# Weight chunks split by two DMA transfers instead of by GpSimd

## The chip, the cores and the metric

The kernel runs on one core of a Trainium2 chip. The metric is device microseconds of one execution, the median over runs; lower is better. The engines are TensorE (PE; its weight loads are listed as PEld), VectorE (DVE), ScalarE (ACT), GpSimd (POOL) and SyncE (SP), each with its own instruction queue. Before the change only SP issues DMA transfers.

## The reference

512 tokens of width 1024 go through three blocks in float32. The first is a gMLP layer with a SwiGLU FFN (hidden width 2816). The second is a FoX attention layer (16 heads of 64, causal softmax with forget gates) with another such FFN. The third is a block of a chunkwise mLSTM beside attention over the 128 best keys of an indexer, then a per-layer-embedding gate and a last norm. Each layer's modulation vectors come from products of `silu(c)` with wide `ada` matrices. Cut to one FFN, which stands for all the large products:

```python
def swiglu(h, w_gu, w_down):
    gu = h @ w_gu
    g, u = jnp.split(gu, 2, axis=-1)
    return (jax.nn.silu(g) * u) @ w_down
```

## The kernel before, in words

**Products in three passes.** A float32 operand f is split exactly into hi, which is f rounded to float32r, and lo = f - hi. A product is then hi*hi + hi*lo + lo*hi, three TensorE instructions (`mm3`, L416 to L418). Activations are split once, when they are transposed to feature-major tiles (`to_T`: ACT at L407, DVE at L408 and L409). Weights are split as they come.

**Weight chunks.** All weight matrices are laid out on the host in chunks of 128 partitions by 1024 columns, 512 KB each. `wsplit` (L273) brings one chunk: `load_w` issues a transfer from SP into a tile `raw` (L271; four buffers), ACT copies it into `whi` with rounding (L279), and a subtraction gives `wlo` (L282). There are four buffers of `whi` and four of `wlo`. A chunk is used in 24 products of 512 columns, and then its `whi` and `wlo` buffers come free. With `share=n` every n-th chunk, by a running count over the whole kernel, has its subtraction on GpSimd and not on DVE; `share=0` means never. 293 chunks go through `wsplit`, 124 of them with the subtraction on GpSimd.

**Where the shares are.** `gemm_a` keeps weights stationary, `gemm_b` keeps activations stationary. In `gemm_a` with `group=4`, the first four chunks go by halves of the tokens (products of 256 columns), since the second half of the tokens is ready later; `gshare=1` puts all four on GpSimd. This is so at the start of both FFNs (gate and up weights `w_gu`, 44 chunks each; afterwards every second chunk in the first FFN, every third in the second) and of the indexer projection `w_ix`. In `gemm_b` with `tail`, the last chunks of a product are held together and used token tile by token tile, so that the first token tiles are finished early; with `head` the whole first group goes so (the last projection, `w_pg`, with `hshare=1`). Values and queries of the FoX layer (`w_vv`, `w_q`) have `share=1`, as have all chunks that `between` places among the attention's steps, and `w_az` and `w_mo`.

**What else uses raw and GpSimd.** Columns of the modulation vectors (`ada`) are loaded into `raw` as well, and DVE multiplies them by `silu(c)` and sums (L302). `fill` places these loads between the chunks; in the first FFN it is two for each chunk from the eleventh on. In the start of the kernel the `ada` columns have tiles of their own (`d`), and DVE, ACT, PE and SP follow an order written out by hand (`manual_schedule`); some chunks are loaded ahead there and given to `wsplit` as `raw=`. Of the chunks with GpSimd's share, four have such a `raw`. GpSimd also adds relative biases and masks to the attention's score tiles (L1132, L1336, L1408), two heads ahead of their use.

**What sets the order.** Outside the part ordered by hand a planner orders the instructions of each queue by its own estimate of when each is ready, in program order among those that are ready. A buffer is taken when the instruction that writes it first is placed. Each queue then runs strictly in that order, and semaphores hold an instruction until its inputs are there.

Of the kernel before, what the change touches and what calls it, by code (L numbers as in the profile page):

```python
"""One-core Trainium2 kernel: a gMLP layer, a FoX attention layer (each with a SwiGLU FFN), then an
mLSTM + indexer-sparse-attention block with a per-layer-embedding gate, for 512 tokens of width 1024.

Large products run as three float32r passes over exactly split operands (hi*hi + hi*lo + lo*hi).
"""
# [55 lines left out]
# ------------------------------------------------------------------ host layout  # L61
def _wa(w):
    """[K, N] -> [N/128, 128 (k in tile), K/128 * 128]: stationary chunks of 128 outputs."""
    k, n = w.shape
    return np.ascontiguousarray(
        w.reshape(k // P, P, n // P, P).transpose(2, 1, 0, 3).reshape(n // P, P, (k // P) * P))


def _wb(w):
    """[K, N] -> [N/512, K/256, 128, 2 * 512]: moving chunks of two k tiles by 512 outputs."""  # L70
# [29 lines left out]
def layout(i):  # L100
# [33 lines left out]
    # gMLP  # L134
# [14 lines left out]
    # FoX  # L149
# [8 lines left out]
    # second block  # L158
# [3 lines left out]
    # rows of the last tile: keys 0-63, input gates 64-67, forget gates 96-99, indexer weights 100-107  # L162
# [28 lines left out]
# ------------------------------------------------------------------ kernel body  # L191
def body(tc, nc, a):
    V, S_, G, PE = nc.vector, nc.scalar, nc.gpsimd, nc.tensor

    with ExitStack() as es:
# [55 lines left out]
        # ---------------- constants  # L251
# [14 lines left out]
        # ---------------- weights: load, split  # L266
# [7 lines left out]
        def wsplit(src, n=1024, share=0, alloc=None, raw=None):  # L274
            """share: every share-th low part on GpSimd"""
            if raw is None:
                raw = load_w(src, n)
            hi, lo = [alloc(F32R) if alloc else tile_of(pw, q, F32R, 1024) for q in ("whi", "wlo")]
            S_.activation(hi[:, 0:n], raw[:, 0:n], AF.Copy)  # L279
            lo_n[0] += 1  # L280
            e = G if share and lo_n[0] % share == 0 else V
            e.tensor_sub(lo[:, 0:n], raw[:, 0:n], hi[:, 0:n].bitcast(F32))  # L282
            return hi, lo

        # ---------------- modulation vectors, worked off between weight chunks
# [21 lines left out]
        def fill(n=1):  # L307
            """one column's load, and the product for the one loaded before"""
# [25 lines left out]
        def gain(csc, gname):  # L334
            """gain * (1 + scale), a column per feature tile"""
# [5 lines left out]
        def gb_row(cg, gname):  # L341
            """gate * gain, on every partition"""
# [13 lines left out]
        # ---------------- norms, transposes  # L356
        def rsq(out, ss, scale):
            """out = 1 / sqrt(ss * scale + eps)"""
            S_.activation(out, ss, AF.Sqrt, bias=epsc[0:out.partition_size(), :], scale=scale)
            V.reciprocal(out, out)  # L360

        def norm_rows(xr, out):
            """out = xr / rms(xr), a token tile in two halves"""
# [8 lines left out]
        def to_T(ts, xn, g, sh, hi, lo, js=range(KD), spill=None):  # L372
            """token-major halves of the tiles ts -> feature-major hi, lo; what is transposed goes
            to spill as well"""
# [39 lines left out]
        # ---------------- products  # L414
# [5 lines left out]
        def gemm_a(h, w, n, evac, m=P, group=0, nfill=0, share=0, gshare=1):  # L420
            """out^T tile i (m outputs by 512 tokens), weights stationary. The first group goes by
            halves of the tokens, since the second half of h comes later."""
# [20 lines left out]
        def gemm_b(h, w, groups, kt, evac, head=False, tail=0, nfill=0, share=0, raws=(), hshare=1):  # L443
            """out tile (g, t): 128 tokens by 512 outputs, activations stationary. The last chunks
            of a group (all of them in the first with head) go token tile by token tile."""
# [25 lines left out]
        def chunks_a(h, w, n, evac):  # L471
            """gemm_a's weight chunks for between(): source, number of steps, step"""
# [15 lines left out]
        def chunks_b(h, w, g, kt, evac):  # L488
            """gemm_b's weight chunks of a group for between()"""
# [17 lines left out]
        def between(chunks, share=1):  # L507
            """products to be placed between the steps of something else: a function that emits the
            next n steps (all that are left without n)"""
# [1107 lines left out]
```

## Time and profile before

| what | value |
|---|---|
| median of 2 runs | 1943.34 us (1941.35 to 1945.34) |
| profiled execution: span, first to last instruction | 1936.7 us (no other time is given for it) |
| mean granted TensorE clock | 0.982 of full speed |
| PE / PEld busy | 1880.1 us (97%) / 1523.1 us (79%) |
| DVE / ACT / POOL busy | 1123.1 us (58%) / 794.6 us (41%) / 375.8 us (19%) |
| DMA | 299.46 MB, mean 155 GB/s, 45.3% of 16 engines' span |

Busy times are sums over one profiled execution; matmuls are pipelined, so PE counts as busy as long as one is under way. The granted clock is the share of 2.4 GHz that the chip gave TensorE in a stretch; its lower level is 1.2 GHz, 0.50. The DMA share is the mean busy share of the core's 16 DMA engines. "Landing" is the time from a transfer's issue to its completion.

### The profile page before, as it was taken

The numbers are of one execution on the slowest core, as the hardware profiler recorded it, in microseconds if no ns is written. First come the engines' busy times: TensorE is split into PE (matmuls) and PEld (weight loads), VectorE is DVE, ScalarE is ACT, GpSimd is POOL, SyncE is SP. The second block draws the span as 40 slices with busy tenths as digits, with TensorE's granted clock in tenths as the row PEclk, the third lists the DMA queues.
The fourth block names the chain that finished last, engine by engine and source line by source line (L and its number), as shares of the span: only waits on it lengthen the run. The fifth ranks groups of instructions, "written<-read, shape, count | busy, mean of one in ns | idle before, by whom it ended". The sixth has DMA issues, their size and how long they took to land.

```text
span 1936.7 us, 23791 instructions
## 1 busy us (share of the span) xinstructions
PE 1880.1 (97%) x8688; PEld 1523.1 (79%) x8688; DVE 1123.1 (58%) x2132; ACT 794.6 (41%) x1395; POOL 375.8 (19%) x216
## 2 busy tenths in 40 slices
PE   7999998999999999999998999999989999999998
PEld 5788877888878877877777888888876877888887
DVE  7879735677762275367757333322365967856534
ACT  5334324422231255477655222222344246455334
POOL 2100123222220013433322111100020353022011
PEclk9999999999999999999998999999987999999999
DMA  8674753477763446733512322233243633322522
GB/s 330 235 274 137 251 194 109 147 265 260 260 219 109 141 138 205 247 120 126 172 67 97 112 94 96 98 109 126 103 136 98 187 129 111 115 93 88 191 96 100
DMA packets 106191, 299.46 MB, mean 155 GB/s; under 512 B 11893, under 2 KB 14749, under 8 KB 106074
## 3 DMA queue, kind: packets, MB, share of 16 engines
q1 hardware_dynamic: 106074, 297.94, 45.3%
q8 instruction: 69, 1.13, 0.2%
q14 instruction: 48, 0.39, 0.1%
HBM read 266.35 MB, written 34.16 MB: 155 GB/s over the span
## 4 chain that ended last, share of the span: by engine, by line
PE 78%; DVE 11%; DMA 7%; issue 2%; ACT 2%; POOL 0%; SPq 0%; DVEq 0%; ACTq 0%
PE acc L416 22%; PE acc L418 22%; PE acc L417 22%; DMA raw<-in_ada 6%; DVE raw L302 3%; PE tp L975 2%; PE tp L1016 2%; DVE d L302 1%; PE tp L1001 1%; PE tp L974 1%; DVE h L408 1%; PE tp L384 1%; DVE wlo L282 1%; DVE h L409 1%; PE tp L815 1%
## 5 line engine op out<-in xcount | busy, mean ns | idle before, releaser
L279 ACT ACTIVATE whi<-raw 128x1024 fp32r<-128x1024 f32 x293 | 309.9, 1059 | 679.4 <-PE acc L418 305.5
L282 POOL TENSOR_TENSOR wlo<-raw,whi 128x1024 fp32r<-128x1024 f32 x124 | 305.1, 2464 | 1368.3 <-ACT whi L279 1189.1
L417 PE MATMUL acc<-h,whi 128*128 128x512 f32 (+1 forms) x1112 | 418.2, 376 | 10.5 <-DVE h L409 10.4
L416 PE MATMUL acc<-h,whi 128*128 128x512 f32 (+1 forms) x1112 | 418.6, 376 | 5.5 <-DVE h L408 5.2
L418 PE MATMUL acc<-h,wlo 128*128 128x512 f32 (+1 forms) x1112 | 417.5, 375 | 3.3 <-DVE wlo L282 2.7
L282 DVE TENSOR_TENSOR wlo<-raw,whi 128x1024 fp32r<-128x1024 f32 x169 | 212.4, 1259 | 312.6 <-ACT whi L279 312.2
L417 PEld LDWEIGHTS acc<-h,whi 128*128 128x128 f32 x1112 | 212.5, 191 | 48.6 <-DVE h L409 12.7
L416 PE MATMUL acc<-whi,h 128*128 128x512 f32 x608 | 242.5, 399 | 7.9 <-DVE h L408 6.5
L416 PEld LDWEIGHTS acc<-h,whi 128*128 128x128 f32 x1112 | 212.8, 191 | 43.2 <-DVE h L408 6.0
L418 PEld LDWEIGHTS acc<-h,wlo 128*128 128x128 f32 x1112 | 212.7, 191 | 41.9 <-DVE wlo L282 4.5
L417 PE MATMUL acc<-wlo,h 128*128 128x512 f32 x608 | 240.0, 395 | 3.2 <-DVE wlo L282 3.2
L418 PE MATMUL acc<-whi,h 128*128 128x512 f32 x608 | 240.8, 397 | 0.0
L302 DVE SCALAR_TENSOR_TENSOR raw<-raw,cact 128x1024 f32<-128x1024 f32 x96 | 148.9, 1562 | 75.4 <-DMA raw<-in_ada 69.8
L416 PE MATMUL acc<-whi,s 128*128 128x512 f32 (+1 forms) x488 | 190.4, 390 | 0.7 <-DVE t L1308 0.7
L417 PE MATMUL acc<-wlo,s 128*128 128x512 f32 (+1 forms) x488 | 190.7, 391 | 0.0
L418 PE MATMUL acc<-whi,s 128*128 128x512 f32 (+1 forms) x488 | 190.2, 390 | 0.0
L416 PEld LDWEIGHTS acc<-whi,h 128*128 128x128 f32 x608 | 115.5, 190 | 34.2 <-DVE h L408 7.6
L417 PEld LDWEIGHTS acc<-wlo,h 128*128 128x128 f32 x608 | 115.2, 189 | 27.0 <-DVE wlo L282 4.1
L418 PEld LDWEIGHTS acc<-whi,h 128*128 128x128 f32 x608 | 115.2, 189 | 26.5 <-DVE h L409 2.4
L416 PEld LDWEIGHTS acc<-whi,s 128*128 128x128 f32 x488 | 91.7, 188 | 20.1 <-DVE t L1308 1.1
L417 PEld LDWEIGHTS acc<-wlo,s 128*128 128x128 f32 x488 | 91.7, 188 | 18.8
L418 PEld LDWEIGHTS acc<-whi,s 128*128 128x128 f32 x488 | 91.7, 188 | 18.6
(349 smaller groups left out, 2416.4 us busy)
## 6 DMA issues: line engine op xcount, KB each, us to landing
raw<-in_ada SPq DMA_DIRECT2D x96, 512.0 KB, 4.3
raw<-in_w_gu SPq DMA_DIRECT2D x88, 512.0 KB, 3.5
raw<-in_w_dn SPq DMA_DIRECT2D x44, 512.0 KB, 3.2
scr<-t SPq DMA_DIRECT2D x60, 256.0 KB, 4.1
raw<-in_w_o SPq DMA_DIRECT2D x20, 512.0 KB, 3.4
row<-scr SPq DMA_DIRECT2D x36, 256.0 KB, 3.4
d<-in_ada SPq DMA_DIRECT2D x16, 512.0 KB, 6.9
raw<-in_w_v SPq DMA_DIRECT2D x16, 512.0 KB, 5.2
```

The costliest lines, as they stand in the source:

```text
L279: S_.activation(hi[:, 0:n], raw[:, 0:n], AF.Copy)
L282: e.tensor_sub(lo[:, 0:n], raw[:, 0:n], hi[:, 0:n].bitcast(F32))
L302: V.scalar_tensor_tensor(raw, raw, 1.0, cact[0], ALU.mult, ALU.mult, accum_out=modc[:, col:col + 1])
L384: PE.transpose(src[:, i * P:(i + 1) * P], xn[t][j // 4][:, (j % 4) * P:(j % 4 + 1) * P], ident[:])
L408: V.tensor_copy(hi[j][:, c], fj)
L409: V.tensor_sub(lo[j][:, c], fj, hi[j][:, c].bitcast(F32))
L416: PE.matmul(out, lh, rh, start=start, stop=False)
L417: PE.matmul(out, lh, rl, start=False, stop=False)
L418: PE.matmul(out, ll, rh, start=False, stop=stop)
L815: PE.matmul(sp[:, n * P:(n + 1) * P], vt[n, i // 4][:, o], rows[i // 4][:, o], start=True, stop=True)
L975: PE.matmul(sp[:, o:o + w], qs_[me, qs], kl[me, 0:w], start=False, stop=True)
L1016: PE.matmul(po[:, s * P:512], vd[s, hd // 4][:, hq * P:(hq + 1) * P], pt[:, PTO[s]:PTO[s] + n], start=(q == 0 and s == 0), stop=(q == 1 an ...
```

## The change

In `wsplit`, a chunk of GpSimd's share that has no `raw` given is no longer loaded by SP. GpSimd issues a transfer from DRAM straight into `whi`, from float32 to float32r. ACT then writes -hi into `wlo`. GpSimd issues a second transfer of the same chunk that adds it onto `wlo`, which leaves f - hi. No `raw` tile is taken for such a chunk. A chunk with `raw` given has its subtraction on DVE whatever its share, and so has every chunk outside the share. All other lines of the diff drop comments.

```diff
         def wsplit(src, n=1024, share=0, alloc=None, raw=None):
-            """share: every share-th low part on GpSimd"""
+            hi, lo = [alloc(F32R) if alloc else tile_of(pw, q, F32R, 1024) for q in ("whi", "wlo")]
+            lo_n[0] += 1
+            if share and lo_n[0] % share == 0 and raw is None:
+                G.dma_start(hi[:, 0:n], src)
+                S_.activation(lo[:, 0:n], hi[:, 0:n].bitcast(F32), AF.Copy, scale=-1.0)
+                G.dma_start(lo[:, 0:n], src, accum_op=ALU.add)
+                return hi, lo
             if raw is None:
                 raw = load_w(src, n)
-            hi, lo = [alloc(F32R) if alloc else tile_of(pw, q, F32R, 1024) for q in ("whi", "wlo")]
             S_.activation(hi[:, 0:n], raw[:, 0:n], AF.Copy)
-            lo_n[0] += 1
-            e = G if share and lo_n[0] % share == 0 else V
-            e.tensor_sub(lo[:, 0:n], raw[:, 0:n], hi[:, 0:n].bitcast(F32))
+            V.tensor_sub(lo[:, 0:n], raw[:, 0:n], hi[:, 0:n].bitcast(F32))
             return hi, lo
```

## Rows read from the trace of the kernel before

**Rows 1.** The page, busy times and shares of the span.
```profile
PE 1880.1 (97%) x8688; PEld 1523.1 (79%) x8688; DVE 1123.1 (58%) x2132; ACT 794.6 (41%) x1395; POOL 375.8 (19%) x216
```

**Rows 2.** The page, the chain of waits by line.
```profile
PE acc L416 22%; PE acc L418 22%; PE acc L417 22%; DMA raw<-in_ada 6%; DVE raw L302 3%; PE tp L975 2%; PE tp L1016 2%; DVE d L302 1%; PE tp L1001 1%; PE tp L974 1%; DVE h L408 1%; PE tp L384 1%; DVE wlo L282 1%; DVE h L409 1%; PE tp L815 1%
```

**Rows 3.** Groups by line: busy us, mean ns, idle before and its releasers.
```profile
L282 POOL TENSOR_TENSOR wlo<-raw,whi 128x1024 fp32r<-128x1024 f32 x124 | 305.1, 2464 | 1368.3 <-ACT whi L279 1189.1 <-DVE t L394 134.5 <-issue 18.0
```

**Rows 4.** Timeline of ACT, second FFN (start us, duration us).
```profile
1082.02 1.06 ACT L279 ACTIVATE whi<-raw 128x1024 fp32r<-128x1024 f32 x1 [3.84 <-PE acc L417]
...
1087.46 1.06 ACT L279 ACTIVATE whi<-raw 128x1024 fp32r<-128x1024 f32 x1 [3.89 <-issue]
```

**Rows 5.** The tile raw, 375 to 565 us: its transfers' landing.
```profile
DMA to landing us min/median/max: 3.2/4.4/6.1
```

**Rows 6.** The page, DMA issues: KB each, median us to landing.
```profile
d<-in_ada SPq DMA_DIRECT2D x16, 512.0 KB, 6.9
```

**Rows 7.** Stages, POOL at L282: start:end, length, busy, count; clock, DMA share, GB/s.
```profile
75.00:320.00 245.00, 27.93 (x11) 0.99 0.59 203
345.00:565.00 220.00, 50.29 (x20) 1.00 0.70 240
742.00:800.00 58.00, 21.55 (x9) 1.00 0.77 247
1045.00:1270.00 225.00, 31.12 (x13) 1.00 0.28 96
```

**Rows 8.** Timeline of DVE, first 75 us.
```profile
22.32 2.23 DVE L708 TENSOR_TENSOR modc<-modc,vecs 128x1 f32<-128x1 f32 x1
...
26.79 1.22 DVE L302 SCALAR_TENSOR_TENSOR d<-d,cact 128x1024 f32<-128x1024 f32 x1
...
29.54 1.23 DVE L282 TENSOR_TENSOR d<-raw,d 128x1024 fp32r<-128x1024 f32 x1
...
62.90 3.40 DVE L302 SCALAR_TENSOR_TENSOR d<-d,cact 128x1024 f32<-128x1024 f32 x1
```

**Rows 9.** Timeline of ACT, group starts and ends, and the last projection.
```profile
321.56 1.09 ACT L279 ACTIVATE whi<-raw 128x1024 fp32r<-128x1024 f32 x1
...
357.74 1.06 ACT L279 ACTIVATE whi<-raw 128x1024 fp32r<-128x1024 f32 x1 [1.34 <-issue]
...
1027.47 1.09 ACT L279 ACTIVATE whi<-raw 128x1024 fp32r<-128x1024 f32 x1
...
1065.78 1.06 ACT L279 ACTIVATE whi<-raw 128x1024 fp32r<-128x1024 f32 x1 [1.34 <-issue]
...
1401.90 1.06 ACT L279 ACTIVATE whi<-raw 128x1024 fp32r<-128x1024 f32 x1
...
1441.08 1.06 ACT L279 ACTIVATE whi<-raw 128x1024 fp32r<-128x1024 f32 x1 [0.58 <-issue]
...
1879.87 1.06 ACT L279 ACTIVATE whi<-raw 128x1024 fp32r<-128x1024 f32 x1 [0.59 <-PE acc L418]
```

**Rows 10.** Timeline of PE, first products of a group and of the last projection.
```profile
1030.47 0.28 PE L416 MATMUL acc<-h,whi 128*128 128x256 f32 x1
...
1882.95 0.48 PE L416 MATMUL acc<-whi,s 128*128 128x512 f32 x1
```

**Rows 11.** Stretches: length, busy of PE, PEld, DVE, ACT, POOL; clock, DMA share, GB/s.
```profile
1036.00:1042.00 6.00, 2.54 (x10) 1.93 (x10) 5.50 (x6) 2.11 (x6) 4.82 (x2) 0.50 0.80 300
425.00:521.00 96.00, 96.00 (x425) 79.51 (x424) 74.75 (x95) 24.51 (x32) 19.29 (x8) 1.00 0.76 261
```

**Rows 12.** Timeline of POOL, first FFN; nine more such rows lie between.
```profile
424.58 2.39 POOL L282 TENSOR_TENSOR wlo<-raw,whi 128x1024 fp32r<-128x1024 f32 x1 [8.88 <-ACT whi L279]
...
546.22 2.40 POOL L282 TENSOR_TENSOR wlo<-raw,whi 128x1024 fp32r<-128x1024 f32 x1 [9.97 <-ACT whi L279]
```

**Rows 13.** Timeline of SP, before the second FFN.
```profile
1004.45 6.35 SPq L271 DMA_DIRECT2D raw<-in_w_gu  x2
1015.33 19.00 SPq L553 DMA_DIRECT2D scr<-hm  x5
```

## The prediction, made before the result was known

> **What bounds the kernel now.** I read the busy times first, then the chain of waits, the groups by line, and the stages one by one. TensorE (PE) is busy 1880.1 of 1936.7 us [rows 1], and the chain is mostly its three passes L416 to L418 [rows 2]: 57 us of idle time, plus what a lowered clock costs, is all that any change could give back. GpSimd's 124 subtractions of L282 take 2464 ns each, 305.1 us, yet GpSimd spends 1189.1 us waiting for ScalarE (ACT) [rows 3]; its speed is not the bound. What the reader is to see is where weights are needed soon after a buffer comes free. In steady stages ACT refills a whi buffer every 1087.46 - 1082.02 = 5.44 us [rows 4]: that is TensorE's time for one chunk (24 products). With four whi buffers, a chunk whose buffer has just come free is needed three chunks later, 3 x 5.44 = 16.3 us. Today 1.06 us of ACT [rows 4] and 2.46 us of GpSimd (3.5 us) follow the release, because the load went ahead into raw. After the change both transfers come after the release. So the prediction compares one chain with 16.3 us, and looks at four places that have no such lead.
>
> **The change, part by part.** The sum is made against the profiled execution (span 1936.7 us). The page gives no other time for it; the median of the two timed runs is 6.6 us above the span, and I add the sum to the median. All of the 124 low parts leave GpSimd: 120 become two transfers, and the four with a raw tile given go to VectorE (DVE).
>
> *The chain.* Neither a rounding transfer nor an accumulating one, nor any transfer issued by GpSimd, is in the trace. The nearest rows are 512 KB loads: landing 3.2 / 4.4 / 6.1 us (least, median, most) in the first FFN [rows 5], 6.9 us for the median of the crowded start [rows 6]. For the first transfer I take 4.4, since it moves what a load moves (bounds 3.2 and 6.9). The second reads the chunk from DRAM and the tile from SBUF, so I take two loads, 8.8 (bounds: one fast load, 3.2; two of the slowest, 13.8). ACT's copy stays at 1.06 us. Chain: 4.4 + 1.06 + 8.8 = 14.3 us, bounds 7.5 and 21.8. At 14.3 it fits into 16.3: **nothing** is lost in the steady stages, and this cover is 2 us thin. Where it fails, each us over the lead costs 53 us, since 11 + 20 + 9 + 13 = 53 such chunks run at full pace [rows 7].
>
> By the fit in the Trainium skill (DMA: Bandwidth & Descriptors, Anatomy of one DMA), 2.0 us plus bytes at 436 GB/s, a 512 KB transfer would take 3.2 us, an estimate, and the chain would be the 7.5 of my lower bound. This trace shows 3.2 us only as the least landing, and for SyncE's queue, so I do not take it.
>
> *Start of the kernel: gain.* DVE orders the first 70 us (four products L302 per feature tile). A product that meets a GpSimd subtraction takes 3.40 us, otherwise 1.22; a one-column add took 2.23 [rows 8]. There are five such meetings, the add being the first and the product of 3.40 the last: 4 x 2.18 + some 2.1 = 10.8 us. Three subtractions of 1.23 us come to DVE there (chunks with raw given; a fourth falls where DVE waits for PE). Net **-7.1 us** (bounds -10.8 and 0: the two chunks that become transfers may be late).
>
> *Three group starts (both FFNs and the indexer projection).* Four chunks, all GpSimd's, follow a tail that holds all four whi buffers to its end. In the second FFN the first buffer is refilled at 1027.47 [rows 9], TensorE wants it at 1030.47 [rows 10], and the group ends at 1065.78 [rows 9]. Today four subtractions stretch DVE's work there, TensorE is busy 2.54 of 6 us in one stretch and is granted a clock of 0.50 in it, 1.2 instead of 2.4 GHz [rows 11]. After: the first low part at 1027.47 + 14.3 = 1041.8, eight half chunks of 2.72 us = 21.8, and 3 us for another such stretch of 6 us at half the clock: 1066.6, so +0.8. In the first FFN 321.56 + 39.1 = 360.7 against 357.74: +3.0; in the indexer 1401.90 + 39.1 = 1441.0 against 1441.08: -0.1 [rows 9]. Together **+3.7 us** (bounds -17 and +26: three times the chain's bounds). The DVE stretching that goes is inside this sum: what is late next is the low part.
>
> *The last projection's head.* TensorE starts it at 1882.95 [rows 10] and reaches the second chunk six products of 0.23 us later; that chunk's buffer is refilled at 1879.87 [rows 9]. Low part at 1894.2, stall 9.9 us plus 3 us of clock: **+12.9 us** (bounds +3 and +20). Here I count no stretched DVE work that would pay it back.
>
> *DMA time.* At a share of 0.76 and 261 GB/s [rows 11] 96 us move 47.8 loads, so one load costs 0.76 x 96 / 47.8 = 1.53 us of all 16 engines. Between 742 and 800 us the share is 0.77 with nine of these chunks [rows 7]: nine accumulations of 2 x 1.53 need 27.5 us, 13.3 are free: **+14 us** (bounds 0 and +28). In the first FFN a pair of chunks carries four ada loads besides; the load side today takes (546.22 - 424.58) / 10 = 12.16 us a pair [rows 12], slower than TensorE's 10.88, and eats the lead, though TensorE is still busy throughout [rows 11]. After: 5 loads, one rounding, one accumulation as two = 8 x 1.53 = 12.2: **0** (bounds: 0, as there is no idle time to win, and +27 with an accumulation of three loads, 17 pairs x 1.6). What pays for it is that raw is wanted five times a pair, not six, and no product meets GpSimd.
>
> *Waits and queues.* GpSimd's queue gets 240 issues; its bias and mask additions for the attention stand behind accumulations that wait for ACT. They run two heads ahead, so I count **0**; without that cover each would cost up to one chain. SyncE loses 120 issues: 0, since what waited there were the loads themselves. ACT's negating copy now waits for a landing, with evacuations queued behind it. The order is not program order: the second FFN's loads were issued at 1004.45, ahead of stores at 1015.33 that stand earlier in the program [rows 13]. So I expect the next first transfer ahead of an accumulation that isn't ready: 0 (bound: the second rival).
>
> Sum: -7.1 + 3.7 + 12.9 + 14 + 0 = +23.5 us, from 1936.7 to 1960 in span, from 1943.3 to **1967 us** in the median, 1.2% slower, which is within the 2% (39 us: 1904 to 1982) that I call no change, about what a measurement here can tell.
>
> **Rivals.**
> *The chain is longer than the lead (slower).* It decides from 16.3 us on. One us over: 53 + 4 starts x 3 = 65 us more, 2032. For it: both transfers' prices are guesses, and 6.1 us landings occur [rows 5]. Against: two loads in a row and the copy still fit at the median. Chance 0.30.
> *GpSimd's queue goes chunk by chunk (slower).* If each accumulation stands ahead of the next first transfer, chunks of a group start come 4.4 + 1.06 = 5.5 us apart instead of 2.72; three gaps of 2.8 at four starts, 33 us: 2000. Against it: [rows 13]. Chance 0.13.
> *GpSimd is locked out while DVE works.* The rows show it between two tensor operations, 2.2 us for the one that comes second [rows 8]. Were both issues held so, the chain would be 18.7: 53 x 2.4 + 4 x 4.4 = 145 us, 2112. The trace has no GpSimd transfer to show it, and a product of 1.22 us would hold it for less. Chance 0.05. The Trainium skill (SBUF — State Buffer, the box on DVE blocking DMA) says that descriptors for such transfers can't be written while DVE runs in a two-port mode; the rows agree on the exclusion only.
> *Accumulation costs what a load costs (faster).* Chain 9.9: starts -9.5, head +8.5, crowded stage +0.5, start -7.1, in sum -8: 1936. For it: the tile's side of the transfer is nowhere a limit in the trace. Chance 0.12.
> *Faster by over 2%:* most idle time and clock loss would have to vanish. 0.03.
> That the transfer doesn't round changes results, not times; it is no case of its own.
>
> **The numbers.** Forecast 0.37, its own range 1950 to 1982. Faster 0.03, same 0.37 + 0.12 = 0.49, slower 0.30 + 0.13 + 0.05 = 0.48. The range runs from 1930 (the cheap accumulation, with the whole gain at the start) to 2060 (1.4 us over the lead); about 2 in 10 lies outside, mostly above.
>
> **What would show it.** Right: no L282 on GpSimd; L302 at 1.2 us throughout the start, which ends some 7 us earlier; ACT's copy about 4.4 us after the first issue, the low part some 9 us later; new TensorE stalls only at group starts and near 1885. Wrong: accumulations landing in over 11 us, TensorE waiting for wlo every third chunk of the second FFN, a DMA share near 1 in the first; or landings near 4 us and a span below 1936.

## The result, and the profile after

The changed kernel takes 2081.22 us (median of two runs, 2079.39 to 2083.05) against 1943.34 us: a ratio of 1.0711 with a 95% interval of 1.0676 to 1.0746, so 138 us slower. That is outside the predicted range of 1930 to 2060 us and far from the forecast of 1967 us. The profiled span is 2081.3 us. Lines behind the edit carry numbers five higher: the passes L416 to L418 are now L421 to L423, the product L302 is L307, the gate's product L582 is L587. In `wsplit` the first transfer is L280, the negating copy L281, the accumulation L282.

The page of the changed kernel first: busy times, the two DMA queues (packets, MB, share of 16 engines' span; q0 holds GpSimd's transfers), and issues with the median us to landing.

```profile
PE 1928.2 (93%) x8688; PEld 1551.6 (75%) x8688; DVE 1022.7 (49%) x2136; ACT 791.2 (38%) x1395; POOL 240.7 (12%) x332
...
q1 hardware_dynamic: 88794, 235.01, 33.0%
q0 software_dynamic: 34560, 125.84, 26.6%
...
raw<-in_ada SPq DMA_DIRECT2D x96, 512.0 KB, 6.0
...
whi<-in_w_gu POOLq DMA_DIRECT2D x41, 512.0 KB, 5.9
wlo<-in_w_gu POOLq DMA_DIRECT2D x41, 512.0 KB, 5.5
...
d<-in_ada SPq DMA_DIRECT2D x16, 512.0 KB, 10.0
```

PE was idle for 57 us of the span before [rows 1] and is for 153 us now. The same products also keep it busy for 48 us more, at a mean granted clock of 0.956 in place of 0.982. In the medians of the largest group, `w_gu`, the first transfer lands in 5.9 us, later than the 4.4 that I had taken, and the accumulation in 5.5, earlier than my 8.8; a start load (`d<-in_ada`) takes 10.0 us where it took 6.9 [rows 6].

To find where the time went, cut both traces at four points that every kernel has: the first and the last L582 (L587) of each FFN, the product of gate and up path on DVE. Timeline of DVE (start us, duration us), before and then after:

```profile
352.12 0.69 DVE L582 TENSOR_TENSOR t<-t,acc 128x512 f32<-128x512 f32 x1 [0.70 <-ACT t L579]
...
580.54 0.69 DVE L582 TENSOR_TENSOR t<-t,acc 128x512 f32<-128x512 f32 x1 [3.38 <-PE tp L347]
...
1060.16 0.69 DVE L582 TENSOR_TENSOR t<-t,acc 128x512 f32<-128x512 f32 x1 [0.70 <-ACT t L579]
...
1283.54 0.69 DVE L582 TENSOR_TENSOR t<-t,acc 128x512 f32<-128x512 f32 x1 [3.37 <-PE tp L347]
```
```profile
358.39 0.69 DVE L587 TENSOR_TENSOR t<-t,acc 128x512 f32<-128x512 f32 x1 [0.75 <-PE acc L423]
...
637.27 0.69 DVE L587 TENSOR_TENSOR t<-t,acc 128x512 f32<-128x512 f32 x1 [3.38 <-PE tp L352]
...
1164.22 0.69 DVE L587 TENSOR_TENSOR t<-t,acc 128x512 f32<-128x512 f32 x1 [0.76 <-PE acc L423]
...
1387.94 0.69 DVE L587 TENSOR_TENSOR t<-t,acc 128x512 f32<-128x512 f32 x1 [3.37 <-PE tp L352]
```

The differences of these rows are the first two lines of a table that the rest of this document uses; the other lines are the same differences in the traces of the experiments below (us; the last column is the profiled span). "Pair" is the mean interval of L587 over ten intervals in the middle of the first FFN.

```
                              to first  first   between  second  behind    span    pair in
                              L587      FFN     the FFNs FFN     it                first FFN
before                        352.1     228.4   479.6    223.4   653.2    1936.7   12.0
after                         358.4     278.9   527.0    223.7   693.4    2081.3   14.9
t4  all low parts on DVE      338.8     223.4   467.8    223.4   643.5    1896.9   11.6
f2  pairs in second FFN only  335.4     223.4   478.7    224.0   645.4    1906.9   11.3
f1  and in the last block     336.0     223.4   479.3    223.8   676.8    1939.3   11.6
d2  dummy rounding            346.2     229.3   472.4    223.4   646.3    1917.6   12.2
d1  dummy accumulation        357.3     256.3   497.8    223.4   662.2    1997.0   13.5
a1  accumulation alone        375.1     266.7   503.2    223.4   664.3    2032.6   14.5
n3  no accumulation           335.7     235.8   484.5    223.4   659.2    1938.5   12.3
t1  accumulate 16 columns     343.7     245.4   502.3    223.4   666.0    1980.7   12.7
t2  second transfer plain     350.4     257.3   500.3    223.4   669.3    2000.6   13.8
h1  accumulate 512 columns    351.4     264.4   520.6    223.4   682.6    2042.4   13.8
n1  PE doesn't wait for it    359.9     275.3   527.1    223.4   678.7    2064.4   14.8
n2  negating copy on GpSimd   372.5     282.0   573.5    228.4   706.2    2162.5   15.6
n4  five raw buffers          352.7     270.4   534.6    224.3   689.1    2071.2   14.8
t3  mask additions on DVE     364.6     282.9   521.3    223.8   678.0    2070.6   15.3
l1  first transfers ahead     368.4     271.7   532.2    224.3   688.5    2085.1   14.5
```

After against before: +6 us to the first FFN, +50 in it, +47 between the FFNs, nothing in the second, +40 behind it; 144.6 us in span, for 138 in the medians. In the first FFN, with a DMA share of 0.70 before [rows 7], the change lost most; in the second, at 0.28, it lost nothing. But behind the second FFN it lost 40 us at a mean share of 0.36 before, so the share alone doesn't sort the stages. Up to the first FFN two things are in the sum: a gain at the start and a larger loss behind it. f2 and f1 do the same work as t4 in the first FFN, and the pair is 11.3 to 11.6 us there: differences of 0.3 us mean nothing.

Inside the first FFN, the stretch that [rows 11] gave for the kernel before (length, busy of PE, PEld, DVE, ACT, POOL, clock, DMA share, GB/s):

```profile
425.00:521.00 96.00, 80.23 (x314) 63.44 (x313) 46.62 (x78) 21.07 (x28) 9.95 (x14) 0.89 0.78 238
```

And the timeline of one pair of chunks there, all engines, with the rows that carry the waits:

```profile
456.42 0.85 POOL L282 DMA_DIRECT2D wlo<-in_w_gu  x1 [13.80 <-ACT wlo L281]
456.97 0.88 POOL L280 DMA_DIRECT2D whi<-in_w_gu  x1
...
458.60 2.08 SPq L303 DMA_DIRECT2D raw<-in_ada  x2
...
463.49 0.80 PE L423 MATMUL acc<-h,wlo 128*128 128x512 f32 x1 [4.93 <-DMA wlo<-in_w_gu]
...
465.97 1.23 DVE L307 SCALAR_TENSOR_TENSOR raw<-raw,cact 128x1024 f32<-128x1024 f32 x1 [5.65 <-DMA raw<-in_ada]
...
469.40 0.68 DVE L587 TENSOR_TENSOR t<-t,acc 128x512 f32<-128x512 f32 x1
470.12 0.63 ACT L532 ACTIVATE s<-t 128x512 fp32r<-128x512 f32 x1 [12.56 <-DVE t L587]
470.66 1.04 ACT L281 ACTIVATE wlo<-whi 128x1024 fp32r<-128x1024 f32 x1
...
471.99 0.85 POOL L282 DMA_DIRECT2D wlo<-in_w_gu  x1 [14.14 <-ACT wlo L281]
472.54 0.87 POOL L280 DMA_DIRECT2D whi<-in_w_gu  x1
```

Two readings fit these rows. PE waits 4.93 us for an accumulation, which came late because the copy stood on ACT behind L532, that behind DVE's L587: a loop through the accumulation (theory A in the expectations). Or: DVE reached L587 late because it waited 5.65 us for an `ada` load, issued at 458.60 behind two transfers of GpSimd, and PE's wait is the consequence (theory B). One more thing stands in these rows: from the first transfer's issue at 456.97 to the next accumulation's at 471.99 are 15.0 us, and that one took 5.4 more to land. From the first transfer's issue to the accumulation's landing, the median over the first FFN's 20 steady chunks is 19.6 us, longer than the lead of 16.3. The wait of the engine that bounds the kernel doesn't say which.

### The profile page after: what moved, and what is told of

The parts are those of the page before. It is cut to its first block, busy times and chain, and to the rows that moved or that the text cites. A ratio compares the mean times of both kernels' runs of the same rounds, so it can differ in the third digit from the quotient of the medians.

```text
span 2081.3 us, 23874 instructions
## 1 busy us (share of the span) xinstructions
PE 1928.2 (93%) x8688; PEld 1551.6 (75%) x8688; DVE 1022.7 (49%) x2136; ACT 791.2 (38%) x1395; POOL 240.7 (12%) x332
## 3 DMA queue, kind: packets, MB, share of 16 engines
q8 instruction: 69, 1.13, 0.2%
## 4 chain that ended last, share of the span: by engine, by line
PE 33%; issue 14%; DMA 5%; POOL 2%; ACT 2%; DVE 1%; POOLq 0%; ACTq 0%; DVEq 0%; SPq 0%
PE acc L423 9%; PE acc L421 9%; PE acc L422 9%; PE tp L980 1%; PE tp L1021 1%; PE tp L1006 1%; DMA whi<-in_w_mo 1%; POOL wlo L282 1%; PE tp L979 1%; DMA whi<-in_w_q 1%; DMA whi<-in_w_g 1%; DMA whi<-in_w_pg 1%; ACT wlo L281 0%; POOL whi L280 0%; DMA wlo<-in_w_pg 0%
## 5 line engine op out<-in xcount | busy, mean ns | idle before, releaser
L423 PE MATMUL acc<-h,wlo 128*128 128x512 f32 (+1 forms) x1112 | 425.3, 383 | 48.6 <-DMA wlo<-in_w_gu 40.6
L421 PE MATMUL acc<-h,whi 128*128 128x512 f32 (+1 forms) x1112 | 424.9, 382 | 8.9 <-DMA whi<-in_w_ix 5.2
L422 PE MATMUL acc<-h,whi 128*128 128x512 f32 (+1 forms) x1112 | 422.2, 380 | 0.0
L286 ACT ACTIVATE whi<-raw 128x1024 fp32r<-128x1024 f32 x173 | 182.6, 1056 | 371.8 <-PE acc L423 199.7
L423 PEld LDWEIGHTS acc<-h,wlo 128*128 128x128 f32 x1112 | 216.3, 195 | 95.5 <-DMA wlo<-in_w_gu 48.3
L421 PE MATMUL acc<-whi,h 128*128 128x512 f32 x608 | 246.8, 408 | 14.5 <-DVE v L892 5.0
L281 ACT ACTIVATE wlo<-whi 128x1024 fp32r<-128x1024 f32 x120 | 126.7, 1057 | 336.1 <-DMA whi<-in_w_gu 66.8
L421 PEld LDWEIGHTS acc<-h,whi 128*128 128x128 f32 x1112 | 217.2, 195 | 47.0 <-DVE sm L554 3.2
L423 PE MATMUL acc<-whi,h 128*128 128x512 f32 x608 | 245.1, 403 | 0.0
L422 PEld LDWEIGHTS acc<-h,whi 128*128 128x128 f32 x1112 | 216.7, 195 | 37.2
L307 DVE SCALAR_TENSOR_TENSOR raw<-raw,cact 128x1024 f32<-128x1024 f32 x96 | 117.2, 1223 | 157.1 <-DMA raw<-in_ada 156.7
L421 PE MATMUL acc<-whi,s 128*128 128x512 f32 (+1 forms) x488 | 191.2, 393 | 0.6 <-DVE t L1313 0.5
L423 PE MATMUL acc<-whi,s 128*128 128x512 f32 (+1 forms) x488 | 191.4, 393 | 0.0
L421 PEld LDWEIGHTS acc<-whi,h 128*128 128x128 f32 x608 | 118.0, 194 | 42.1 <-ACT v L890 5.4
L423 PEld LDWEIGHTS acc<-whi,h 128*128 128x128 f32 x608 | 118.0, 194 | 26.2 <-DVE h L414 1.3
L532 ACT ACTIVATE s<-t 128x512 fp32r<-128x512 f32 x57 | 35.9, 629 | 217.9 <-DVE t L587 201.5
L421 PEld LDWEIGHTS acc<-whi,s 128*128 128x128 f32 x488 | 92.2, 189 | 20.8 <-DVE t L1313 0.9
```

Source lines behind the costliest of these rows:

```text
L281: S_.activation(lo[:, 0:n], hi[:, 0:n].bitcast(F32), AF.Copy, scale=-1.0)
L307: V.scalar_tensor_tensor(raw, raw, 1.0, cact[0], ALU.mult, ALU.mult, accum_out=modc[:, col:col + 1])
L421: PE.matmul(out, lh, rh, start=start, stop=False)
L422: PE.matmul(out, lh, rl, start=False, stop=False)
L423: PE.matmul(out, ll, rh, start=False, stop=stop)
L532: S_.activation(h, f, AF.Copy, scale=scale)
```

## The experiments

All were timed against the kernel before on the same chip; its median was 1940.5 to 1944.7 us there, so differences between experiments carry some 4 us.

**n1: PE doesn't wait for the accumulation.** `return hi, hi` in place of `return hi, lo` behind the accumulation.

> TensorE reads the high part in place of the low part for the chunks that GpSimd's transfers fill, so nothing waits for the accumulation any more; both transfers, the negating copy and every queue stay as they are. Changed kernel: 15.0 us from one pair of chunks to the next in the middle of the first FFN (L587, mean of 425.54 to 515.59), 2081 us. Theory A (in the first FFN the wait of TensorE for the accumulation closes the loop: evacuation, negating copy, accumulation, products): a pair falls to 12.2 us or less, that stage gives back some 56 us, total about 2020. Theory B (there the loop goes through the four raw buffers: ada loads land later beside the two transfers, VectorE waits for them, and TensorE's wait is only its consequence): a pair stays at 14.5 to 15.5 us, total 2055 to 2081, with what comes back only outside the first FFN.

Measured 2057.68 us, ratio 1.0583 (1.0556 to 1.0610). In the first FFN the pair stays at 14.8 us, and PE's waits from 420 to 640 us (us, times, longest) become:

```profile
PE acc L423 <- DVE wlo L287: 28.0, 12, 4.1
```

In the changed kernel that row read `DMA wlo<-in_w_gu`, 33.2 us. The wait moved to the chunks that come through raw: both kinds of chunk are late, and theory A falls. The wait for the low part is worth 24 us in all, 3.6 of them in the first FFN.

**n2: the negating copy on GpSimd.** `G.tensor_scalar_mul(lo, hi, -1.0)` for the activation L281.

> The negating copy goes from ScalarE to GpSimd, so it stands behind no evacuation; the two transfers stay. GpSimd waits for the landing itself. Theory A (the copy comes late because it stands behind ScalarE's evacuation): a pair in the first FFN falls to 12.2 us or less; total about 2020. Theory B (raw buffers and landings): a pair stays at 14.5 us or more in the first FFN. Theory C, for the attention's projections w_vv and w_q (GpSimd's queue goes chunk by chunk: next first transfer, behind the accumulation, behind the copy, behind the landing): no gain there, since the copy is in that same queue: 9 to 11 us a chunk as now. B and C together: 2075 to 2120 (a copy of some 2 us on GpSimd, 120 times, partly on the path).

Measured 2156.58 us, ratio 1.1101 (1.1070 to 1.1133), slower than even the expectation. The first FFN takes 282.0 us. Freeing the copy from ACT's queue gains nothing there, which gives A no support; but it is no clean test, since the copy takes 2.87 us on GpSimd for 1.06 on ACT and stands in the queue of the transfers.

**n3: no accumulation.** The line L282 is deleted.

> The accumulation is left out (the low part is only minus the high part, so the output is not the reference's); first transfer and negating copy stay. It takes away 63 MB of transfers, 26.6% / 2 of the engines' time, and the wait at once. Theory A and theory B both give the first FFN back (pair at 12.2 us or less): A since the chain is 5.5 us shorter, B since the ada loads have the queues to themselves for longer. Together with the run in which only the wait is gone it tells the two apart. Total about 1960 to 2000: the second transfer is most of the loss. If the loss is the first transfer's late start (it waits for the whi buffer, where the load into raw went ahead), 2040 or more.

Measured 1940.91 us, ratio 0.9986 (0.9971 to 1.0001): without the second transfer the whole loss is gone, lower than I expected. Its q0 row gives the price of a first transfer:

```profile
q0 software_dynamic: 17280, 62.92, 10.6%
```

0.106 x 1938.5 / 120 = 1.71 us of all 16 engines. With both transfers it is 0.266 x 2081.3 = 553.6 us, so an accumulation takes (553.6 - 205.5) / 120 = 2.90 us.

**n4: five raw buffers.** `RAW = 5`, and `NZ = 25` to make room.

> Five raw buffers in place of four (and one tile fewer of 26 in the z pool of the last block, to make room). Nothing else changes. Theory B (first FFN: ada loads go round four raw buffers, and each landing is later): each buffer's turn may take a quarter longer, so a pair falls from 15.0 to 12.0 to 13 us, first FFN 35 us or more shorter, total 2035 to 2050. Theory A (accumulation on TensorE's path): a pair stays at 15 us, total 2075 to 2085. If the queues of the DMA are simply full there: 15 us as well, with a share near 1.

Measured 2077.16 us, ratio 1.0695 (1.0652 to 1.0738). A miss: the pair stays at 14.8 us, where B expected 12 to 13. `raw<-in_w_gu` lands in 4.4 us where it took 3.3, `raw<-in_ada` in 4.9 where it took 6.0, and the pair doesn't follow. So neither loop, A's through the accumulation nor B's through the four raw buffers, sets the pair by itself; the runs below vary what is left, the accumulation's time on the DMA engines and its place in GpSimd's queue.

**t1: the accumulation covers 16 columns.** `G.dma_start(lo[:, 0:16], src[:, 0:16], accum_op=ALU.add)`.

> The accumulation stays where it is in GpSimd's queue, with its wait for the negating copy, but covers 16 of 1024 columns (the other columns of these low parts keep minus the high part). What goes is its time on the DMA engines (348 us of all 16, worked out from 26.6% of 2081 with it and 10.6% of 1938 without it); what stays is each place where GpSimd's queue waits for ScalarE with first transfers and mask additions behind it. Theory D (the DMA engines' time and the later landings of everything else): total 1935 to 1965, as without the accumulation (1941). Theory Q (GpSimd's in-order queue): total 2030 to 2065, as with the low part's wait taken from TensorE (2058). The two may share: the attention stage between the FFNs (last L587 of the first to first L587 of the second: 479.6 us before, 526.9 changed, 484.5 without accumulation) says it for itself: near 485 for D, near 527 for Q.

Measured 1984.31 us, ratio 1.0217 (1.0186 to 1.0248), between the two: 97 us of the 138 go with the accumulation's size (D), and 43 us remain over n3 for its place in the queue, the waits and the small transfer itself (Q at most). Between the FFNs, 502.3 us: 25 us D, 18 Q.

**t2: the second transfer rounds and overwrites.** `G.dma_start(lo[:, 0:n], src)`, without `accum_op`.

> The second transfer rounds and overwrites in place of accumulating (the low part is then the high part again): same bytes from DRAM, same queue, same waits, 1.7 in place of 2.9 us of the 16 engines' time each. Theory D: 120 x 1.2 us = 144 us of DMA time less; a good half of the loss comes back, 1970 to 2010. Theory Q, or a loss by the number and the waits of transfers: 2050 to 2081.

Measured 2000.19 us, ratio 1.0308 (1.0276 to 1.0341), as D expected: the same bytes from DRAM and the same queue, and 81 us less than with accumulation.

**t3: mask additions on DVE.** `V.tensor_add` for `G.tensor_add` at L1137, L1341 and L1413.

> The mask and bias additions of the three attentions (L1137, L1341, L1413) go from GpSimd to VectorE, so nothing but weights stands in GpSimd's queue. Theory Q (attention waits for additions stuck behind an accumulation): the stage between the FFNs falls from 527 towards 490 and what follows the second FFN by some 15 to 25 us, total 2020 to 2050. Theory D: within 10 us of 2081, perhaps slower by the time that VectorE spends on them (60 x 0.7 us at most).

Measured 2067.55 us, ratio 1.0627 (1.0590 to 1.0664). In all 14 us, not the 30 to 60 that Q needed, but the stages differ. Behind the second FFN 15 us go, as Q expected there; between the FFNs 6, where Q expected some 37; and up to the end of the first FFN, where no mask is added, this run takes 10 us more, which stays unexplained.

**t4: all low parts on DVE.** In the kernel before, `e = V`.

> The kernel before with all low parts on VectorE and none on GpSimd (loads through raw as before). VectorE gets 124 x 1.22 = 151 us and loses the stretching by GpSimd's subtractions (2.2 us a meeting). If those meetings are what the change was good for, it gains at the start as the run without accumulation did (first L587 at 335.7 against 352.1 us) and ends at 1915 to 1940; if VectorE was short of time in the first FFN and the attention, 1945 to 1980.

Measured 1898.85 us, ratio 0.9777 (0.9761 to 0.9792): faster than both kernels and than either expectation. Having the subtractions on GpSimd had cost 44 us all along. The page of this kernel:

```profile
PE 1866.7 (98%) x8688; PEld 1514.4 (80%) x8688; DVE 1152.9 (61%) x2256; ACT 793.0 (42%) x1395; POOL 74.4 (4%) x92
```

DVE takes on 124 subtractions, and its busy time rises by 30 us only [rows 1], since its other work is no longer stretched.

**d1: dummy accumulations.** In t4's kernel, beside each of the 120 chunks and with nothing reading `dum` (shortened; `dum` is a tile made for this):

```diff
+            if share and lo_n[0] % share == 0 and given is None:
+                G.tensor_copy(dum[:, 0:1], hi[:, 0:1].bitcast(F32))
+                G.dma_start(dum[:, 0:n], src, accum_op=ALU.add)
```

> The kernel with all low parts on VectorE (1899 us), and beside each of the 120 chunks an accumulating transfer of the same 512 KB onto a tile that no product reads; a one-column copy on GpSimd of the chunk's high part sets the moment (it also holds the whi buffer until then; one z tile fewer makes the room). Only the transfers' time is added to work that doesn't wait for them. Theory D (the DMA engines' time, 2.9 us of all 16 for each accumulation, makes the other loads late): 1975 to 2010, about what the accumulation of 1024 in place of 16 columns cost (97 us), most of it at the start, in the first FFN and between the FFNs. If accumulations only cost where something waits for them: 1899 to 1915.

Measured 1999.93 us, ratio 1.0319 (1.0288 to 1.0350): 101 us for transfers that no product waits for. In this trace ACT waits 29.7 us for GpSimd's one-column copies, which hold whi buffers. The next run has the same copies and tells what they can cost.

**d2: the same with plain transfers.** d1 without `accum_op`.

> As d1 (all low parts on VectorE, and 120 transfers of 512 KB onto a tile that no product reads), but the dummy transfers round and overwrite, they don't accumulate. Same bytes from DRAM, same queue, same moments; 1.7 in place of 2.9 us of the 16 engines' time each. If the loss goes with that time alone: 101 x 1.7 / 2.9 = 59 us, 1950 to 1965. If the accumulating transfers hurt by more than their time (with the low parts waiting, 1.4 us more of plain transfer cost 16 us, the next 1.2 us of accumulating 81): 1900 to 1935.

Measured 1923.24 us, ratio 0.9907 (0.9883 to 0.9932): 24 us over t4. The q0 rows of d1 and of d2:

```profile
q0 software_dynamic: 17280, 62.92, 18.6%
```
```profile
q0 software_dynamic: 17280, 62.92, 10.1%
```

0.186 x 1997.0 / 120 = 3.10 us, and 0.101 x 1917.6 / 120 = 1.61 us, for the same bytes from DRAM. The loss is 101 to 24 where these times are 3.10 to 1.61: more than in proportion. ACT waits 13.7 us for the copies here, 16 less than in d1, so of the 77 us between the two runs some 60 at least come from accumulating as such.

**h1: half accumulations.** `lo[:, 0:n // 2]` and `src[:, 0:n // 2]` in the accumulation.

> The changed kernel with accumulations over 512 of 1024 columns (the other half of these low parts keeps minus the high part). 16 columns: 1984 us, 1024 columns: 2081. Loss in proportion to the columns: 2025 to 2040. If the engines have room until a certain load and then no more: 1990 to 2015 for the half, the rest for the second half.

Measured 2046.35 us, ratio 1.0528 (1.0507 to 1.0549). Half the columns bring 62 of the 97 us: neither proportion nor a threshold. But it makes a pair with t2: its q0 share is 19.9% of 2042.4 us, t2's 20.1% of 2000.6 us, so, with 1.71 us for each first transfer, the second takes 1.67 and 1.64 us of the engines. In the first FFN both run at 13.8 us a pair; between the FFNs h1 is 20 us longer. For the same time of the engines its other loads land later than t2's: `raw<-in_w_gu` in 4.5 us for 3.2, `raw<-in_ada` in 5.7 for 5.0.

**a1: the accumulation alone.** The chunk is loaded through raw and rounded by ACT as before; ACT writes minus the high part, and GpSimd accumulates.

> One part of the change alone: the chunk is loaded ahead into raw and rounded by ScalarE as before, ScalarE makes minus the high part (120 more copies of 1.06 us), and GpSimd's transfer accumulates onto it. Per chunk 1.53 + 2.9 us of the DMA engines against 1.7 + 2.9 in the changed kernel; the lead of the raw load is back. Theory D: the accumulation keeps costing what it cost, 2000 to 2045; what the late first transfer costs by itself (1941 without accumulation against 1899 with none of it, 42 us) comes back. If the late start of the first transfer and the chunk-by-chunk queue were the main loss: 1940 to 1980.

Measured 2025.59 us, ratio 1.0453 (1.0417 to 1.0489), as D expected. The raw load in place of the first transfer is worth 56 us against the changed kernel, and more behind the start, which is 17 us longer here.

**l1: the next first transfer ahead.** `wsplit` cut in two, the next chunk's first half written ahead of this chunk's second (shortened):

```diff
+                    start(c + 1)
+                    wh, wl = wfinish(sts[c])
-                    wh, wl = wsplit(w[gi, c], share=share, ...)
```

> Same work as the changed kernel, but the next chunk's first transfer is written ahead of this chunk's copy and accumulation (and all four ahead of the four copies at a group's tail), so that in GpSimd's queue in w_vv and w_q first transfers stand ahead of accumulations. Theory Q (the order in GpSimd's queue): the stage between the FFNs falls from 527 to some 505 to 512 (the part that the 16-column accumulation left over the run without one is 18 us), total 2045 to 2065. Theory D alone: within 10 us of 2081.

Measured 2088.75 us, ratio 1.0785 (1.0750 to 1.0820). Between the FFNs it takes 532.2 us, no shorter. But the run doesn't test what it was to test. The planner orders each queue by its own estimate, and in the trace the 16 transfers of `w_vv`, and those of `w_q`, stand in GpSimd's queue in the same order as in the changed kernel (first transfer H, accumulation L): HLHHLHLHLLHLHHLL and HHLHLHLLHLHHLLHL in both. What that order costs stays open; with the short accumulation it is a part of the 43 us that t1 keeps over n3.

**f1 and f2: transfer pairs in the second FFN only.** A switch set around that FFN's first product; in f1 a later variable of the same name turned it on again for the last block.

> Transfer pairs only in the second FFN's gate and up projection (17 chunks), all other low parts on VectorE (that kernel: 1899 us). The DMA engines are half idle there and ScalarE's copy comes in time. If the chain of transfer, copy and accumulation fits into the lead of three chunks, as the prediction had it: 1897 to 1906 us, L587 of the second FFN 10.88 us apart as ever, at most 5 us lost at its group start. If the chain itself is too long: 53/4 us or more for each us over the lead, 1915 and up.

f1 measured 1941.43 us, ratio 1.0006 (0.9989 to 1.0022). With 26 chunks of the last block as transfer pairs (the trace has 43 pairs, 17 of them in the FFN; the 21 in the next expectation is a miscount) it doesn't test what it was to test; f2 does. Against f2 it shows something else: those 26 pairs cost 34 us, 31 of them behind the second FFN (676.8 us for 645.4).

> f1 as it was meant: in f1 the switch was overwritten further down, and the last block's 21 later chunks were transfer pairs as well. Here only the 17 chunks of the second FFN's gate and up projection are; all other low parts on VectorE (that kernel: 1899 us). The prediction's cover (a chain that fits into three chunks) holds: pairs of L587 10.88 us apart in that FFN, and the loss is the group start alone, which took some 9 us in f1's trace: 1903 to 1914. The 28 us that f1 lost behind the second FFN are not there. If steady chunks cost something too: 1920 or more.

f2 measured 1907.26 us, ratio 0.9814 (0.9795 to 0.9834): 8 us over t4, as expected. A steady stretch of that FFN (columns as above):

```profile
1042.00:1260.00 218.00, 217.68 (x965) 180.10 (x964) 61.18 (x69) 65.10 (x81) 17.82 (x25) 1.00 0.48 129
```

PE is busy in all of it but 0.3 us. One chunk in f2, timeline (its L281 to L283 are the transfer, copy and accumulation), and the landing of the tile wlo's accumulations:

```profile
1081.96 0.56 POOL L281 DMA_DIRECT2D whi<-in_w_gu  x1 [10.25 <-PE acc L424]
...
1085.57 1.06 ACT L282 ACTIVATE wlo<-whi 128x1024 fp32r<-128x1024 f32 x1 [3.04 <-DMA whi<-in_w_gu]
...
1086.92 0.86 POOL L283 DMA_DIRECT2D wlo<-in_w_gu  x1 [4.40 <-ACT wlo L282]
```
```profile
DMA to landing us min/median/max: 5.2/5.4/6.3
```

From 1081.96 to 1086.92 + 5.4 = 1092.3 are 10.4 us, well inside 16.3; the first transfer's median landing in this stretch is 3.7 us.

## Why the prediction was wrong, point by point

**Where the 138 us come from.** Four kernels form a chain. Taking the low parts off GpSimd: -44 (1943 to 1899, t4). Adding accumulations that nobody needs: +101 (d1). Needing them, with ACT's extra copy: +26 (a1). Replacing the raw load by a first transfer that can't start before the buffer is free: +56 (2081). The largest item is what accumulating transfers cost even where nothing waits for them. In d1 other loads land later (`raw<-in_w_gu` in 5.1 us for t4's 3.5, `raw<-in_ada` in 5.2 for 4.3); but time on the DMA engines alone doesn't account for the loss (d1 beside d2, h1 beside t2).

**The step that failed: "DMA time", first FFN, 0.** Measured there: +50 us. The price was right: I took 1.53 and 3.06 us of the engines for the two transfers, and the runs show 1.71 and 2.90 (that it comes from reading both chunk and tile, as I argued, no run shows). A pair then needs 5 x 1.53 + 1.71 + 2.90 = 12.3 us of engine time, as predicted. But I compared it with the 12.16 us interval of [rows 12] and found cover. The interval was no engine time: six loads need 6 x 1.53 = 9.2 us, which is the 0.76 of [rows 11] once more. In the other 2.9 us of each pair the engines are not busy, yet this time didn't serve as room: added engine time came on top of it, and a fit of 12.3 into 12.2 would have needed engines without a gap (the highest share of any run over these intervals is 0.90, in d2).

```
        engine time of a pair                 measured pair   difference
before  6 x 1.53                  =  9.2      12.0            2.8
n3      5 x 1.53 + 1.71           =  9.4      12.3            2.9
t1      9.36 + 0.29               =  9.6      12.7            3.1
t2, h1  9.36 + 1.64, 1.67         = 11.0      13.8            2.8
after   9.36 + 2.90               = 12.3      14.9            2.6
```

(t1's 0.29 is (0.121 x 1980.7 - 205.5) / 120. By the DMA share of the ten intervals themselves, 0.75 and 0.79, the engine time is 9.0 before and 11.8 after, the same to half a us.) In the kernels that load every chunk through raw the difference is smaller (2.4 in t4, 2.3 in a1, 1.4 in d2, 1.3 in d1), so the sum holds for the kernel before and the changed kernel's kind alone. With "before plus 3.1" in place of "fits into 12.2" the step would have given 15.1 us a pair and, over some 16 pairs, 50 us: what was lost, though this sum is made after the fact. What fills the 2.6 to 3.1 us is not shown. Round trips are likely (a product ends, a load goes out, lands, and DVE's next product can start), but a fifth raw buffer, which should have hidden some, changed nothing (n4). The Trainium skill (DMA: Bandwidth & Descriptors, SWDGE vs HWDGE vs iDMA) says that transfers issued by GpSimd and those of other queues feed different queues inside each engine, which serves them in turn. The traces are in keeping with that and don't test it: SyncE's `ada` loads land in 4.4 us without the accumulation (n3) and in 6.0 with it.

**One crowded stretch was checked, three were there.** I counted DMA time between 742 and 800 us (+14). I gave no DMA term to the rest of w_vv and w_q, nor to the 11 chunks from 75 to 320 us [rows 7]. The DMA view of the changed kernel in the stretch of w_vv and w_q, 813 to 932 us (busy tenths of 40 slices; then queues as above), and that of before in 747 to 862 us:

```profile
DMA  8999928899999999999918990899999907926990
...
q0 software_dynamic: 4464, 16.25, 57.3%
q1 hardware_dynamic: 6043, 11.22, 28.0%
```
```profile
DMA  8887076989789992385547899514130432470055
...
q1 hardware_dynamic: 9766, 22.72, 58.8%
```

The two are not the same work: before, the loads of w_vv and w_q were issued from 732 to 816 us, and the emptier second half of its view holds those of w_g; now the same loads and their accumulations go out from 813 to 932 us, with no such half. What PE did in the two stretches (columns as above), before and then after:

```profile
747.00:862.00 115.00, 112.22 (x503) 88.08 (x503) 56.02 (x150) 61.96 (x109) 49.26 (x22) 1.00 0.59 198
```
```profile
813.00:932.00 119.00, 99.40 (x410) 78.42 (x408) 33.99 (x76) 45.19 (x70) 24.67 (x34) 0.91 0.86 232
```

It gets through 410 products where it got through 503, at a clock of 0.91. On the same work, counted by PE's matmul instructions, the 500 that took 115 us before (741 to 856) take 144 now (808 to 952): +29 of the 47 us between the FFNs.

**Start, predicted -7.1.** The meetings are gone as said; DVE's group in the first 70 us is

```profile
L307 DVE SCALAR_TENSOR_TENSOR d<-d,cact 128x1024 f32<-128x1024 f32 x16 | 18.9, 1218 | 0.0
```

with a mean of 1218 ns, where [rows 8] had one of 3.40 us. The last of these products starts at 56.0 us, before at 66.2, though the loads for them land in 10.0 us. Counted by PE's matmul instructions, the changed kernel reaches the 240th at 67.6 us, 8.2 earlier than before (75.8), and so does t4: the start was forecast right. The gain is lost behind it, in stretches that I had at 0: 6.8 us of it between 94 and 130 us, while t4 keeps most of its lead and reaches the first L582 13 us earlier.

**What else GpSimd's subtractions cost.** I looked for it at the start and at the group starts alone. t4 shows 44 us over the whole kernel. Had I priced it, the forecast would have been lower still: a further miss of the other sign.

**The chain against the lead, predicted 0: right in the second FFN alone.** There it is 10.4 us, not 14.3 (the accumulation lands in 5.4 us where I took 8.8), and steady chunks cost nothing (223.4 and 223.7 us). In the first FFN the chain is 19.6 us in the median, over the lead, as the first rival had it: one chain time for all stages was wrong. Yet the rival's reason doesn't hold either, for with PE's wait for the low part gone the pair stays (n1). In the prediction, the fit in the Trainium skill (DMA: Bandwidth & Descriptors, Anatomy of one DMA) gave 3.2 us a transfer, an estimate. The first transfer's 3.7 us in the second FFN of f2 is near it, the accumulation's 5.4 is not.

**Group starts, +3.7: too low, but inside the bounds.** In the second FFN 34.0 us pass from the first refill (issue at 1130.22) to the first L587, where it was 32.7 from 1027.47 [rows 9]: +1.3 for +0.8. In the first FFN 35.2 for 30.6: +4.6 for +3.0. In the indexer 36.1 us pass from the first refill (1505.97) to the next ACT copy into whi behind the group (1542.06), for 30.5 before: +5.5 for -0.1. Together some +11. **Last projection, +12.9: too high.** PE waits 4.0 us there for the low part, for 9.9 predicted: the chain is 12.4 us for 14.3, and PE has 5.7 us of other work before it needs that low part, where I counted 1.4.

**Waits and queues, 0: partly wrong.** At the first FFN's group start the four first transfers do go ahead of the accumulations (323.23 to 328.34, then 333.08). In the FFN's steady stretch the next first transfer goes behind the accumulation (471.99, then 472.54), against what I read from [rows 13]; what that costs no run separates, and all that t1 keeps over n3 is 43 us. Mask additions behind accumulations, counted 0, do cost: counted by PE's matmul instructions, some 18 of the 40 us behind the second FFN are lost in the last block's attention over the indexer's keys, and some 7 with these additions on DVE (t3). The lock-out rival: GpSimd's issues took 0.53 to 1.13 us each, where that rival had 2.2 us more for each; nothing here speaks for it.

**What stays open.** What GpSimd's queue order costs: l1 left it as it was. Why an accumulation costs more than its engine time outside the first FFN: t2 and h1 take the same time of the engines, yet h1 is 46 us slower, 20 of it between the FFNs. How much of a1's step to the changed kernel is the late start and how much ACT's and GpSimd's order was not separated.

## What to carry to other kernels

A DMA price belongs to every stretch where loads are on the path, and that it fits into the interval measured there doesn't show that it is covered. Here, at a share of 0.76, all of it came on top in the changed kernel's kind; in t4's first FFN, at 0.83 over the ten intervals, 1.6 us more a pair (d2) made the pair 0.6 us longer and the share 0.90. So free DMA time may or may not be room: take the price as fully added for one bound, and test it. And before work is moved from a slow engine to a new mechanism, run it on the engine that has time: here the plain subtraction on VectorE was faster than both.

## What the runs showed of the hardware

For 512 KB from DRAM, a transfer of GpSimd that rounds took 1.6 to 1.7 us of the 16 engines' time, one that accumulates 2.9 to 3.1 us; landing in the second FFN 3.7 and 5.4 us in the median. Their issues occupy GpSimd 0.55 and 0.85 us. An accumulation of 16 columns still took 0.29 us of the engines. With no GpSimd tensor operations beside it, DVE's 128x1024 product takes 1218 ns in the mean; in a meeting with a GpSimd subtraction it took 2.2 us more [rows 8]. Moving all 124 subtractions to DVE was worth 44 us net; how much of that is the meetings was not separated.
